# Output and down projection with tokens on the partitions and the weights moving, and a seam to the gate stage by token tile

## The chip, the cores and the metric

The kernel runs on one core of a Trainium2 chip. Its engines work side by side, each through its own list of instructions: PE (TensorE, matmuls; PEld is its load of the operand that stays in the array), DVE (VectorE), ACT (ScalarE), POOL (GpSimd) and SP (SyncE, which here issues the weight loads). The metric is the device time of one execution in microseconds, the median of three runs. The profile is of one execution; its span is the time between the first and the last thing that the profiler saw.

## The reference

One layer over 256 latent tokens of width 2048 (and 256 context tokens that only feed the state of the token mixer). All arithmetic is in float32. What the change touches is the end of the token mixer, the second norm and the feed-forward block:

```python
hx = modulate(rmsnorm(x, norm_mix[l]), sh1, sc1)
x_parts, _, _ = mixer_front(hx, w_in[l], ...)
x = x + g1 * mixer_back(x_parts, ..., w_proj_a[l], w_proj_b[l], w_out[l])   # ends in "@ w_out"
hx = modulate(rmsnorm(x, norm_ffn[l]), sh2, sc2)
x = x + g2 * swiglu(hx, w_ffn_gate[l], w_ffn_up[l], w_ffn_down[l])
...
return rmsnorm(x, norm_final)
```

The vectors sh, sc and g come from SiLU(c) times a matrix w_mod of 2048 by 12288, plus b_mod. w_out is 2048 by 2048, gate and up are 2048 by 5632, down is 5632 by 2048. The mixer's input projection and its state scan come first.

## The kernel before, in words

Every large product is split to keep float32 precision: an operand is taken apart into a rounded part (hi) and the rest (lo), and hi x hi, lo x hi and hi x lo are summed in PSUM. Activations lie with their channels on the partitions: a tile such as `mx` or `h2` holds, for each block of 128 channels, the hi and the lo part of 256 tokens side by side. So one matmul with a 128 by 128 block of weights as the loaded operand and 512 columns moving does hi x hi and lo x hi at once, in two halves of a PSUM bank; one with 256 columns adds the lo part of the weights (`mm_unit`, lines 151 and 153). `fold` then adds the two halves, with a copy on ACT and an addition on DVE.

Weights come in units of 512 KB: `w32` loads a unit with SP (six buffers), `split` makes its hi part on ACT (line 113) and its lo part on DVE (line 114), into four buffers each. `split` is moved some 450 instructions ahead of its place in the program by a priority, so that units are ready before PE asks. `pair` runs one pair of 128 output channels through all units of a weight matrix. With `whole` set it keeps 256 columns to a matmul and needs no fold (lines 143, 144 and 146); this is done for the last pair of the output and of the down projection.

The vectors of the second half (g1, sh2, sc2, g2) are computed beside other stages by `modvec`: DVE multiplies rows of w_mod by one number per partition and sums (line 493), PE adds over the partitions (line 499), ACT copies (501), PE transposes (504), and DVE adds the bias into `modc`, one number per partition. A generator is advanced from `hook`, once per weight unit and by a fixed ratio, so that this work is spread over the stages.

The stages around the change, in order:
- At the start (p0), x is transposed on PE, and ACT copies its 256 token columns to a buffer `ev` from which POOL writes them to `xT_d` (lines 393 and 394), block by block.
- The output projection (pd) has eight calls of `pair`; x comes back from `xT_d`, DVE forms x1 = x + g1 * y (line 951), ACT the squares, and POOL writes x1 to `x1_d`.
- The seam into the gate stage: PE sums the squares over the partitions (line 968) and spreads the scale back over them (976); then DVE, ACT, ACT and DVE make each of 16 blocks of `h2` (lines 978 to 985). The gate stage (pe) starts its first matmuls block by block.
- The down projection (pf) is like the output projection, with x1 read back, and with four transposes per pair (line 1052) that put the result back with tokens on the partitions for the output. The final norm's scale comes at the end (1044 to 1047), then the scaling and the six output writes.

Each engine has one list of instructions, ordered by the program and the priorities; the buffers of a pool are handed on in that order.

## Time and profile before

| | |
|---|---|
| median of 3 runs | 2410.69 us (2408.48 to 2411.11) |
| the profiled execution | 2409.69 us |
| its span | 2407.9 us |
| PE busy | 2346.0 us, 97% of the span |
| DVE busy | 1639.7 us, 68% |
| ACT busy | 1266.5 us, 53% |
| moved by DMA | 509.41 MB, 212 GB/s on average |

Busy times are averages over stages with different limits; the table by stage in the rows below is read first. Durations of matmuls overlap, so their cost is read from the distance between starts.

### The profile page before, as it was taken

The numbers are of one execution on the slowest core, as the hardware profiler recorded it, in microseconds if no ns is written. First come the engines' busy times: TensorE is split into PE (matmuls) and PEld (weight loads), VectorE is DVE, ScalarE is ACT, GpSimd is POOL, SyncE is SP. The second block draws the span as 40 slices with busy tenths as digits, with TensorE's granted clock in tenths as the row PEclk, the third lists the DMA queues.
The fourth block names the chain that finished last, engine by engine and source line by source line (L and its number), as shares of the span: only waits on it lengthen the run. The fifth ranks groups of instructions, "written<-read, shape, count | busy, mean of one in ns | idle before, by whom it ended". The sixth has DMA issues, their size and how long they took to land.

```text
span 2407.9 us, 35235 instructions
## 1 busy us (share of the span) xinstructions
PE 2346.0 (97%) x13400; PEld 1976.3 (82%) x13400; DVE 1639.7 (68%) x2134; ACT 1266.5 (53%) x1980; POOL 131.2 (5%) x165
## 2 busy tenths in 40 slices
...
GB/s 280 289 280 139 134 135 153 160 125 162 136 148 155 163 199 192 266 264 282 246 267 295 261 282 251 276 288 190 219 231 223 210 230 225 222 193 193 192 192 114
DMA packets 468457, 509.41 MB, mean 212 GB/s; under 512 B 18147, under 2 KB 438194, under 8 KB 467776
## 3 DMA queue, kind: packets, MB, share of 16 engines
...
## 4 chain that ended last, share of the span: by engine, by line
PE 84%; DMA 7%; issue 4%; DVE 4%; ACT 2%; POOL 0%; SPq 0%; DVEq 0%; ACTq 0%; POOLq 0%
PE acc L151 38%; PE acc L153 20%; PE acc L143 6%; PE acc L144 6%; PE acc L146 6%; DMA w<-in_w_mod_dram 4%; PE acc L155 2%; DVE wl L114 2%; PE ss L667 1%; DMA cs<-cs_d 1%; PE ss L637 1%; PE tp L558 1%; PE ss L370 1%; DMA w<-in_w_in_dram 1%; DMA yst<-yg_d 1%
## 5 line engine op out<-in xcount | busy, mean ns | idle before, releaser
L114 DVE TENSOR_TENSOR wl<-w,wh 128x1024 fp32r<-128x1024 f32 (+3 forms) x702 | 847.2, 1211 | 486.0 <-ACT wh L113 484.8
L113 ACT CAST wh<-w 128x1024 fp32r<-128x1024 f32 (+3 forms) x702 | 717.0, 1023 | 703.8 <-PE acc L151 459.4
L151 PE MATMUL acc<-hx,wh 128*128 128x512 f32 x1556 | 433.0, 397 | 0.0
L151 PE MATMUL acc<-h,wh 128*128 128x512 f32 x1320 | 366.9, 397 | 4.7 <-DVE h L985 2.4
L151 PEld LDWEIGHTS acc<-hx,wh 128*128 128x128 f32 x1556 | 271.6, 189 | 40.9 <-issue 2.6
L153 PEld LDWEIGHTS acc<-hx,wl 128*128 128x128 f32 x1664 | 254.8, 188 | 35.6
L143 PE MATMUL acc<-hx,wh 128*128 128x512 f32 x656 | 265.7, 406 | 4.1 <-ACT wh L113 3.0
L153 PE MATMUL acc<-hx,wl 128*128 128x256 f32 x1664 | 264.9, 281 | 0.0
L151 PEld LDWEIGHTS acc<-h,wh 128*128 128x128 f32 x1320 | 231.5, 190 | 38.9 <-issue 4.5
L144 PE MATMUL acc<-hx,wh 128*128 128x512 f32 x656 | 259.2, 396 | 0.0
L153 PEld LDWEIGHTS acc<-h,wl 128*128 128x128 f32 x1408 | 215.9, 189 | 30.1
L493 DVE SCALAR_TENSOR_TENSOR mac<-w,silc,mac 128x1024 f32<-128x1024 f32 x120 | 154.7, 1289 | 120.2 <-DMA w<-in_w_mod_dram 119.8
L153 PE MATMUL acc<-h,wl 128*128 128x256 f32 x1408 | 223.7, 281 | 0.0
L146 PE MATMUL acc<-hx,wl 128*128 128x512 f32 x656 | 184.2, 394 | 0.0
L151 PE MATMUL acc<-hid,wh 128*128 128x512 f32 x602 | 166.3, 396 | 0.0
L143 PEld LDWEIGHTS acc<-hx,wh 128*128 128x128 f32 x656 | 123.8, 189 | 39.8 <-ACT wh L113 7.9
L146 PEld LDWEIGHTS acc<-hx,wl 128*128 128x128 f32 x656 | 123.9, 189 | 27.8 <-DVE wl L114 0.8
L144 PEld LDWEIGHTS acc<-hx,wh 128*128 128x128 f32 x656 | 124.2, 189 | 25.7 <-issue 1.6
L151 PE MATMUL acc<-yg,wh 128*128 128x512 f32 x496 | 136.6, 395 | 0.0
L151 PEld LDWEIGHTS acc<-hid,wh 128*128 128x128 f32 x602 | 103.6, 189 | 13.8
L153 PEld LDWEIGHTS acc<-hid,wl 128*128 128x128 f32 x616 | 94.4, 189 | 13.1
L618 ACT ACTIVATE cs<-cs,ncs 128x128 f32<-128x128 f32 x256 | 81.6, 390 | 32.4 <-DMA cs<-cs_d 30.6
...
## 6 DMA issues: line engine op xcount, KB each, us to landing
...
```

The lines of the kernel that those rows point to most:

```text
L113: A.copy(out=hi[:, :n], in_=t[:, :n])
L114: V.tensor_tensor(out=lo[:, :n], in0=t[:, :n], in1=hi[:, :n].bitcast(F32), op=ALU.subtract)
L143: E.matmul(o, wj(hi, k), act(kofs + k)[:, 0, :ncol], start=kofs + k == kbeg, stop=False)
L144: E.matmul(o, wj(hi, k), act(kofs + k)[:, 1, :ncol], start=False, stop=False)
L146: E.matmul(o, wj(lo, k), act(kofs + k)[:, 0, :ncol], start=False, stop=last and k == nk - 1)
L151: E.matmul(o2, wj(hi, k), act(kofs + k)[:, :, :T], start=kofs + k == kbeg, stop=False)
L153: E.matmul(o[:, :T], wj(lo, k), act(kofs + k)[:, 0, :T], start=False, stop=last and not hold)
L155: E.matmul(o2, wj(hi, nk - 1), act(kofs + nk - 1)[:, :, :T], start=False, stop=True)
L370: E.matmul(b[32 * j:32 * j + 32, :fb], sil[:, rr, :], wt[:, r, :], start=rr < 4, stop=rr >= KD - 4)
L493: V.scalar_tensor_tensor(out=ac, in0=wt, scalar=silc[:, k - 1:k], in1=ac, op0=ALU.mult, op1=ALU.add)
L558: E.transpose(out=b[:, i * P:(i + 1) * P], in_=v, identity=ident)
L618: A.activation(out=t4[:, r, j], in_=t4[:, r, j], func=AF.Identity, bias=ncs[:, cc, r * 64 + hs + j:r * 64 + hs + j + 1])
```

## The change

- The output and the down projection have the activations as the loaded operand and the weights moving: a PSUM tile holds 128 tokens by up to 512 output channels. The 2048 output channels go in chunks of 512, 512, 512, 256 and 256 (`CHUNKS`), and a unit holds 2 or 4 blocks of 128 input channels (`mm_tok`, `chunks`). There is no fold and no transpose of the down projection's result.
- g1 and g2 are needed along the free dimension now: `modvec` writes them as a row to `gr_d`, adds the bias before the sum over the partitions, and skips the transposes for them; they are read back spread over all partitions. `modvec` has one more step in each half, between the copy and what follows.
- x is read where it is needed, from the input; `xT_d` and its writes at the start are gone. x1 and the output are token by channel.
- Norms: squares are summed along the free dimension by the instruction that makes them, with one scale per partition.
- The seam: the last chunk of the output projection runs all its units for token tile 0 first, then for tile 1 with the same held weight buffers. The norm of a tile (`norm2`) scales, transposes on PE and evicts with scale and bias, four blocks at a time. The first four gate units run for tile 0 and then, again with held buffers, for tile 1 (`mm_half`), ahead of the up units.

```diff
+CHUNKS = (512, 512, 512, 256, 256)
...
-    xT_d = dpool.tile([P, KD, T], F32, name="xT_d")
-    x1_d = dpool.tile([P, KD, T], F32, name="x1_d")
+    x1_d = dpool.tile([T, D], F32, name="x1_d")
+    gr_d = dpool.tile([2, D], F32, name="gr_d")
...
+    def mm_half(a, hi, lo, nk, kofs, kend, act, tt):
+
+        s = slice(tt * P, (tt + 1) * P)
+        for j in range(2):
+            o = a[j].rearrange("p (h t) -> p h t", h=2)[:, :, s]
+            wj = lambda t, k: t[:, k, j * P:(j + 1) * P]
+            for k in range(nk):
+                E.matmul(o, wj(hi, k), act(kofs + k)[:, :, s], start=kofs + k == 0, stop=False)
+            for k in range(nk):
+                E.matmul(o[:, 0], wj(lo, k), act(kofs + k)[:, 0, s], start=False, stop=kofs + k == kend - 1)
+
+    def mm_tok(a, hi, lo, nk, kofs, kend, act, tt):
+
+        s = slice(tt * P, (tt + 1) * P)
+        o = a[tt][:, :UB // nk]
+        for k in range(nk):
+            E.matmul(o, act(kofs + k)[:, 0, s], hi[:, k], start=kofs + k == 0, stop=False)
+            E.matmul(o, act(kofs + k)[:, 1, s], hi[:, k], start=False, stop=False)
+        for k in range(nk):
+            E.matmul(o, act(kofs + k)[:, 0, s], lo[:, k], start=False, stop=kofs + k == kend - 1)
+
+    def chunks(w, ktot, act, epi, hook=None, split=False):
+
+
+        c0 = 0
+        for j, n in enumerate(CHUNKS):
+            a, nk = acc2(), UB // n
+            held = []
+            for k in range(0, ktot, nk):
+                u = (*unit_cols(w, k, nk, [(c0, n)]), nk, k, ktot, act)
+                for tt in range(1 if split and j == len(CHUNKS) - 1 else 2):
+                    mm_tok(a, *u, tt)
+                held.append(u)
+                if hook is not None:
+                    hook()
+            epi(a, 0, j, c0, n)
+            if split and j == len(CHUNKS) - 1:
+                for u in held:
+                    mm_tok(a, *u, 1)
+            epi(a, 1, j, c0, n)
+            c0 += n
...
-                xo = p0.tile([P, 512], F32, tag="ev", name="ev", bufs=2)[:, :T]
-                A.copy(out=xo, in_=b[:, :T])
-                nc.gpsimd.dma_start(out=xT_d[:, k, :], in_=xo)
...
+            if slot in (0, 3):
+                br = w32([(lambda t: t[0:1, :], b_mod[0][c0:c0 + UB].rearrange("(a n) -> a n", a=1))])
...
                     V.tensor_scalar(out=ac, in0=wt, scalar1=silc[:, 0:1], scalar2=None, op0=ALU.mult)
+                    if slot in (0, 3):
+                        V.tensor_tensor(out=ac[0:1, :], in0=ac[0:1, :], in1=br[0:1, :], op=ALU.add)
...
             A.copy(out=ev, in_=b[:, :w])
+            yield
+            if slot in (0, 3):
+                nc.gpsimd.dma_start(out=gr_d[slot // 3, h * UB:(h + 1) * UB].rearrange("(j n) -> j n", j=4),
+                                    in_=ev.rearrange("(j r) n -> j r n", j=4)[:, 0, :])
+                continue
...
-    hook = bg(mgen, 102, 226)
+    hook = bg(mgen, 108, 226)
...
-        x1 = pd.tile([P, KD, T], F32, name="x1")
-        ss2 = pd.tile([P, 2, T], F32, name="ss2")
-        for j in range(8):
-            xr = pd.tile([P, 2, T], F32, tag="xr", name="xr", bufs=2)
-            nc.gpsimd.dma_start(out=xr, in_=xT_d[:, 2 * j:2 * j + 2, :])
-            a = pair(w_out, j * 256, KD, lambda k: mx[:, k], hook, whole=j == 7)
...
-            if j < 7:
-                fold(a, t)
...
-                v = (ss2, t)[i // 2][:, i % 2, tt * P:(tt + 1) * P]
-                E.matmul(b[:, 2 * tt:2 * tt + 2], v, ones[:, 0:2], start=i == 0, stop=i == 3)
...
+        x1 = [pd.tile([P, D], F32, name=f"x1{i}") for i in range(2)]
+        g1 = pd.tile([P, D], F32, name="g1")
+        sq = pd.tile([P, 2, len(CHUNKS)], F32, name="sq")
+        rs2 = pd.tile([P, 2], F32, name="rs2")
+        nc.gpsimd.dma_start(out=g1, in_=gr_d[0].partition_broadcast(P))
+        xr = {}
+
+        def xload(j):
+            c0, n = sum(CHUNKS[:j]), CHUNKS[j]
+            xr[j] = pd.tile([P, 2, 512], F32, tag="xr", name="xr", bufs=2)
+            nc.gpsimd.dma_start(out=xr[j][:, :, :n], in_=x[:, c0:c0 + n].rearrange("(t p) n -> p t n", p=P))
+
+        def norm2(tt):
+
+            r = rs2[:, tt:tt + 1]
+            V.tensor_reduce(out=r, in_=sq[:, tt, :], op=ALU.add, axis=mybir.AxisListType.X)
+            A.activation(out=r, in_=r, func=AF.Sqrt, scale=1.0 / D, bias=eps_t)
+            V.reciprocal(out=r, in_=r)
+            for k0 in range(0, KD, 4):
+                xn = pd.tile([P, 512], F32, tag="xn", name="xn", bufs=2)
+                V.tensor_scalar(out=xn, in0=x1[tt][:, k0 * P:k0 * P + 512], scalar1=r, scalar2=None, op0=ALU.mult)
+                b = tpb()
+                for i in range(4):
+                    E.transpose(out=b[:, i * P:(i + 1) * P], in_=xn[:, i * P:(i + 1) * P], identity=ident)
+                h = pd.tile([P, 4, P], F32, tag="h32", name="h32", bufs=2)
+                for i in range(4):
+                    k = k0 + i
+                    bi = b[:, i * P:(i + 1) * P]
+                    if i % 2:
+                        A.activation(out=h[:, i, :], in_=bi, func=AF.Identity, scale=modc[:, 2, k:k + 1],
+                                     bias=modc[:, 1, k:k + 1])
+                    else:
+                        V.tensor_scalar(out=h[:, i, :], in0=bi, scalar1=modc[:, 2, k:k + 1],
+                                        scalar2=modc[:, 1, k:k + 1], op0=ALU.mult, op1=ALU.add)
+                hh, hl = (h2[:, k0:k0 + 4, i, tt * P:(tt + 1) * P] for i in range(2))
+                A.copy(out=hh, in_=h)
+                V.tensor_tensor(out=hl, in0=h, in1=hh.bitcast(F32), op=ALU.subtract)
+
+        def epi(a, tt, j, c0, n):
+            last = j == len(CHUNKS) - 1
+            if tt == 0 and not last:
+                xload(j + 1)
+            if tt == 0 and last:
+                for _ in mgen:
+                    pass
+            cs = slice(c0, c0 + n)
+            xc, xt = x1[tt][:, cs], xr[j][:, tt, :n]
+            V.tensor_tensor(out=xc, in0=a[tt][:, :n], in1=g1[:, cs], op=ALU.mult)
+            V.tensor_tensor(out=xc, in0=xc, in1=xt, op=ALU.add)
+            if last:
+                V.scalar_tensor_tensor(out=xt, in0=xc, scalar=1.0, in1=xc, op0=ALU.mult, op1=ALU.mult,
+                                       accum_out=sq[:, tt, j:j + 1])
             else:
...
+                A.activation(out=xt, in_=xc, func=AF.Square, accum_out=sq[:, tt, j:j + 1])
+            nc.gpsimd.dma_start(out=x1_d[tt * P:(tt + 1) * P, cs], in_=xc)
+            if last:
+                norm2(tt)
+        xload(0)
+        chunks(w_out, KD, lambda k: mx[:, k], epi, hook, split=True)
...
-        hook = bg(mgen, 34, 168)
+        hook = bg(mgen, 36, 168)
+        h2a = lambda k: h2[:, k]
         for j in range(KF // 2):
             ag, au = acc2(), acc2()
+            if j == 0:
+                held = []
+                for k0 in range(0, KD, UK):
+                    held.append((*unit_cols(w_gate, k0, UK, [(0, 256)]), UK, k0, KD, h2a))
+                    mm_half(ag, *held[-1], 0)
+                    hook()
+                for u in held:
+                    mm_half(ag, *u, 1)
             for k0 in range(0, KD, UK):
                 for w, a in ((w_gate, ag), (w_up, au)):
-                    hi, lo = unit_cols(w, k0, UK, [(j * 256, 256)])
-                    mm_unit(a, hi, lo, UK, k0, KD, [0, 0], lambda k: h2[:, k])
-                    hook()
+                    if j or a is au:
+                        hi, lo = unit_cols(w, k0, UK, [(j * 256, 256)])
+                        mm_unit(a, hi, lo, UK, k0, KD, [0, 0], h2a)
+                        hook()
...
-            a = pair(w_down, j * 256, KF, lambda k: hid[:, k], whole=j == 7)
-            t = pf.tile([P, 2, T], F32, tag="ff", name="ff", bufs=2)
-            if j < 7:
-                fold(a, t)
...
+        g2 = pf.tile([P, D], F32, name="g2")
+        nf = pf.tile([P, D], F32, name="nf")
+        sq = pf.tile([P, 2, len(CHUNKS)], F32, name="sq3")
+        rs = pf.tile([P, 2], F32, name="rsf")
+        nc.gpsimd.dma_start(out=g2, in_=gr_d[1].partition_broadcast(P))
+        nc.gpsimd.dma_start(out=nf, in_=norm_final.partition_broadcast(P))
+        for tt in range(2):
+            nc.gpsimd.dma_start(out=ot[tt], in_=x1_d[tt * P:(tt + 1) * P, :])
+
+        def epi3(a, tt, j, c0, n):
+            last = j == len(CHUNKS) - 1
+            cs = slice(c0, c0 + n)
+            o = ot[tt][:, cs]
+            t = pf.tile([P, 512], F32, tag="ff", name="ff", bufs=2)[:, :n]
+            V.tensor_tensor(out=t, in0=a[tt][:, :n], in1=g2[:, cs], op=ALU.mult)
+            V.tensor_tensor(out=o, in0=o, in1=t, op=ALU.add)
+            if last:
+                V.scalar_tensor_tensor(out=t, in0=o, scalar=1.0, in1=o, op0=ALU.mult, op1=ALU.mult,
+                                       accum_out=sq[:, tt, j:j + 1])
             else:
...
+                A.activation(out=t, in_=o, func=AF.Square, accum_out=sq[:, tt, j:j + 1])
+                V.tensor_tensor(out=o, in0=o, in1=nf[:, cs], op=ALU.mult)
+        chunks(w_down, KF, lambda k: hid[:, k], epi3)
+        V.tensor_reduce(out=rs, in_=sq, op=ALU.add, axis=mybir.AxisListType.X)
+        A.activation(out=rs, in_=rs, func=AF.Sqrt, scale=1.0 / D, bias=eps_t)
+        V.reciprocal(out=rs, in_=rs)
...
+                    V.scalar_tensor_tensor(out=ot[tt][:, m:], in0=ot[tt][:, m:], scalar=r, in1=nf[:, m:], op0=ALU.mult,
+                                           op1=ALU.mult)```

How the instructions stand, at three places. First PE where a gate vector is summed over the partitions, for g1. Before (`mac` is the vector, `ident` the operand of a transpose; L151, L153 and L155 are matmuls of the projection that runs there):

```order
L155 MATMUL acc<-hx,wh 128x512
L499 MATMUL tp<-mac,ones 32x256 x4
L151 MATMUL acc<-hx,wh 128x512 x4
L153 MATMUL acc<-hx,wl 128x256
L504 MATMUL tp<-ident,mac 128x128 x2
L153 MATMUL acc<-hx,wl 128x256 x3
```

The same place now (L543 is the sum over the partitions; L152, L154 and L156 are the old L151, L153 and L155):

```order
L156 MATMUL acc<-hx,wh 128x512
L543 MATMUL tp<-mac,ones 32x256 x4
L152 MATMUL acc<-hx,wh 128x512 x4
L154 MATMUL acc<-hx,wl 128x256 x4
L152 MATMUL acc<-hx,wh 128x512 x4
```

The two transposes of this half have gone.

Second, PE at the seam. Before, from the last matmuls of the output projection (L146) over the sums and the spread scale to the first gate matmuls (`h_13993` is `h2`):

```order
L146 MATMUL acc<-mx,wl 128x256 x4
L968 MATMUL tp<-ones,ss_13998 128x2 x2
L968 MATMUL tp<-ones,fd 128x2 x2
L968 MATMUL tp<-ones,ss_13998 128x2 x2
L968 MATMUL tp<-ones,fd 128x2 x2
L976 MATMUL tp<-dg,ones 128x128 x2
L151 MATMUL acc<-h_13993,wh 128x512 x10
L153 MATMUL acc<-h_13993,wl 128x256 x4
```

Now, from inside the last unit of token tile 1 (L174, L175 and L177 are `mm_tok`, L1012 the transposes of `norm2`, L165 and L167 `mm_half`, `h_13945` is `h2`):

```order
L174 MATMUL acc<-wh,mx 128x256
L1012 MATMUL tp<-ident,xn 128x128 x8
L175 MATMUL acc<-wh,mx 128x256
L174 MATMUL acc<-wh,mx 128x256
L175 MATMUL acc<-wh,mx 128x256
L174 MATMUL acc<-wh,mx 128x256
L175 MATMUL acc<-wh,mx 128x256
L174 MATMUL acc<-wh,mx 128x256
L175 MATMUL acc<-wh,mx 128x256
L177 MATMUL acc<-wl,mx 128x256 x4
L1012 MATMUL tp<-ident,xn 128x128 x8
L165 MATMUL acc<-h_13945,wh 128x2x128 x4
```

Two sets of eight transposes stand ahead of the first gate matmul, the second directly ahead of it. Those of token tile 1 stand inside the gate units of tile 0.

Third, DVE at the same place, now, from the last operation of tile 0's epilogue on (L115 is the lo split of a weight unit, L1009 the normalised block `xn`, L1021 an eviction of a transposed block, L1036 the epilogue of tile 1, L1025 the lo part of `h2`):

```order
L1039 SCALAR_TENSOR_TENSOR xr,sq<-x_13949 128x256
L1004 TENSOR_REDUCE rs_13953<-sq 128x1
L115 TENSOR_TENSOR wl<-w_14860,wh 128x1024
L1006 RECIPROCAL rs_13953<-rs_13953 128x1
L1009 TENSOR_SCALAR xn<-x_13949,rs_13953 128x512 x2
L115 TENSOR_TENSOR wl<-w_14882,wh 128x1024
L115 TENSOR_TENSOR wl<-w_14904,wh 128x1024
L1021 TENSOR_SCALAR h_14685<-tp,modc 128x128
L1021 TENSOR_SCALAR h_14699<-tp,modc 128x128
L115 TENSOR_TENSOR wl<-w_14926,wh 128x1024
L1021 TENSOR_SCALAR h_14685<-tp,modc 128x128
L1021 TENSOR_SCALAR h_14699<-tp,modc 128x128
```

Before, the reciprocal had one split ahead of it, and the blocks of `h2` followed it:

```order
L114 TENSOR_TENSOR wl<-w_15045,wh 128x1024
L971 RECIPROCAL rs_14891<-rs_14891 128x4
L975 TENSOR_SCALAR dg<-ident,rs_14891 128x128 x2
L978 SCALAR_TENSOR_TENSOR x_13997<-x_13997,modc,tp 128x256 x2
L981 TENSOR_SCALAR x_13997<-x_13997,modc 128x256
L978 SCALAR_TENSOR_TENSOR x_13997<-x_13997,modc,tp 128x256 x2
L985 TENSOR_TENSOR h_13993<-x_13997,h_13993 128x256 x2
```

All four gate units' splits stand among the operations of tile 0's norm now, three ahead of its first evictions and the fourth between them.

## Rows read from the trace of the kernel before

**Rows 1.** Busy time by stage: engine busy us (instructions), granted clock, DMA share, GB/s.

```profile
0.00:180.00 180.00, 146.51 (x1068) 99.64 (x1069) 95.18 (x200) 65.64 (x139) 18.11 (x41) 0.96 0.92 283
...
1553.00:1637.00 84.00, 82.77 (x508) 73.17 (x508) 57.79 (x75) 37.89 (x52) 8.05 (x15) 1.00 0.85 269
...
1637.00:1656.00 19.00, 15.11 (x79) 12.91 (x79) 15.36 (x34) 13.61 (x29) 0.55 (x1) 0.82 0.40 123
...
2145.00:2396.40 251.40, 251.40 (x1524) 222.86 (x1523) 126.11 (x139) 103.95 (x123) 4.00 (x8) 1.00 0.56 176
```

**Rows 2.** DMA of the first 180 us: bytes; one issue group (count, KB, landing us).

```profile
DMA packets 54219, 50.95 MB, mean 283 GB/s; under 512 B 2470, under 2 KB 53167, under 8 KB 53693
...
xT_d<-ev POOLq DMA_DIRECT2D x14, 128.0 KB, 5.3
```

**Rows 3.** Waits in the first 180 us: waiter <- waited for: us, times, longest.

```profile
ACT ev L374 <- DMA xT_d<-ev: 4.3, 2, 3.6
```

**Rows 4.** Groups by line, PE, whole span: busy us, mean ns, idle before, releaser.

```profile
L504 PE MATMUL tp<-ident,mac 128*128 128x128 f32 x16 | 3.2, 279 | 3.3 <-ACT mac L501 3.3
```

**Rows 5.** PE in order of time, 410 to 2192 us: start, us, instruction.

```profile
411.44 0.39 PE L144 MATMUL acc<-hx,wh 128*128 128x512 f32 x1
...
413.98 0.84 PE L151 MATMUL acc<-hx,wh 128*128 128x512 f32 x3
...
2180.26 0.70 PE L1052 MATMUL tp<-ident,xr 128*128 128x128 f32 x4
...
2180.72 0.72 PE L153 MATMUL acc<-hid,wl 128*128 128x256 f32 x4
...
2182.19 0.64 PE L153 MATMUL acc<-hid,wl 128*128 128x256 f32 x4
...
2182.66 1.09 PE L151 MATMUL acc<-hid,wh 128*128 128x512 f32 x4
...
2190.61 0.64 PE L153 MATMUL acc<-hid,wl 128*128 128x256 f32 x4
```

**Rows 6.** PE in order of time at the seam into the gate stage.

```profile
1636.25 0.64 PE L146 MATMUL acc<-mx,wl 128*128 128x256 f32 x4
...
1638.17 0.59 PE L968 MATMUL tp<-ones,ss 128*128 128x2 f32 x4
...
1638.62 0.59 PE L968 MATMUL tp<-ones,fd 128*128 128x2 f32 x4
...
1643.30 4.60 PE L151 MATMUL acc<-h,wh 128*128 128x512 f32 x10 [2.44 <-DVE h L985]
...
1647.71 0.67 PE L153 MATMUL acc<-h,wl 128*128 128x256 f32 x4
```

**Rows 7.** Groups by line, PE, from 1636.5 to 1655.24 us.

```profile
L151 PE MATMUL acc<-h,wh 128*128 128x512 f32 x29 | 10.2, 480 | 2.4 <-DVE h L985 2.4
...
L153 PE MATMUL acc<-h,wl 128*128 128x256 f32 x28 | 4.5, 282 | 0.0
```

**Rows 8.** Groups by line, DVE, from 1300 us on.

```profile
L114 DVE TENSOR_TENSOR wl<-w,wh 128x1024 fp32r<-128x1024 f32 x378 | 460.0, 1222 | 299.2 <-ACT wh L113 298.6 <-PE acc L151 0.4
...
L896 DVE TENSOR_TENSOR mx<-fc,mx 128x512 fp32r<-128x512 f32 x8 | 5.5, 683 | 0.0
...
L951 DVE SCALAR_TENSOR_TENSOR x<-fd,modc,xr 128x256 f32<-128x256 f32 x14 | 6.8, 484 | 4.9 <-DMA xr<-xT_d 4.5
...
L1064 DVE TENSOR_SCALAR ot<-ot,rsf 128x512 f32<-128x512 f32 x2 | 1.0, 484 | 0.0
...
L975 DVE TENSOR_SCALAR dg<-ident,rs 128x128 f32<-128x128 f32 x2 | 0.5, 284 | 0.0
```

**Rows 9.** Groups by line, ACT, from 1300 us on.

```profile
L113 ACT CAST wh<-w 128x1024 fp32r<-128x1024 f32 x378 | 395.8, 1050 | 460.6 <-PE acc L151 344.2 <-PE acc L155 46.7 <-issue 32.3
```

**Rows 10.** Order of time at the end, PE and DVE.

```profile
2395.78 0.64 PE L146 MATMUL acc<-hid,wl 128*128 128x256 f32 x4
...
2399.28 1.41 DVE L1064 TENSOR_SCALAR ot<-ot,rsf 128x512 f32<-128x512 f32 x3
```

78 lines of the change are left out of this document (5 added, 73 removed).

## The prediction

> **What bounds the kernel now.** I read the table by stage first. TensorE (PE) is the bound: in the down projection it is busy for all of 251.4 us, in the output projection for 82.8 of 84 us [rows 1]. Two stretches differ. In the first 180 us PE is busy for 146.5 us while the DMA engines are at 0.92: there the bytes set the pace. Between the output projection and the first full-speed gate matmuls PE waits for VectorE (DVE). So I asked three things: what a matmul costs in the new form, what the two seams (into the gate stage, and to the end) cost PE, and what becomes of the DMA traffic of the first 180 us. After the stages I read the DMA queues of the first stretch, PE in order of time at one place of each form, and the seam in order of time.
>
> **The matmuls.** Back to back, eleven 512-column matmuls take 413.98 - 411.44 = 2.54 us, 0.231 each; four 256-column ones take 0.47, 0.12 each [rows 5]. A unit in the old form (8 of 512 and 8 of 256 columns) is 2 x (2190.61 - 2182.19)/6 = 2.807 us [rows 5]. In the new form a 512-column chunk has 12 matmuls of 512 columns a unit, 2.772; a 256-column chunk has 24 of 256, 2.88, which is also what the last pair costs now. Which operand is loaded and which moves makes no difference to the row I can see; the columns do. Output projection before: 28 x 2.807 + 4 x 2.88 = 90.1; after: 24 x 2.772 + 8 x 2.88 = 89.6: **-0.5**. Down projection before: 77 x 2.807 + 11 x 2.88 = 247.8, after: 66 x 2.772 + 22 x 2.88 = 246.3: -1.5. It also loses its transposes: four took 2180.72 - 2180.26 = 0.46 of PE's time, seven such sets lay between matmuls, -3.2 [rows 5]. Down in all **-4.7**; PE is never idle there, so this comes off the path whole. Bounds: if a 512-column matmul with moving weights went at 0.234, both stages would gain nothing from the form, +3.
>
> **The gate vectors.** The rows for g1 and g2 are no longer transposed on PE. The sixteen transposes of line 504 cost 0.115 each of PE's time and 3.3 us of idle time for the copy just before them [rows 4]. Eight of them go; the other eight now stand a hook later, with matmuls in between, as the order shows. -0.9 and -3.3: **-4.2**, or -0.9 if the idle time only moves to the next weights. Added on DVE are four additions on one partition and on the weight queue four 4 KB loads that hold one of six buffers each for two hooks. They lie beside matmuls that have four split units in hand; I cost them at nothing, +1 if that cover is thin. The two new writes of a gate row sit between two uses of the one "mac" buffer; the next use comes a hook later (about 6 us), against 5.3 us for a write on that queue [rows 2].
>
> **The first 180 us.** The write of the transposed x goes: 14 writes of 128 KB in this stretch are 1.8 MB of 50.95 MB. At 283 GB/s that is 6.5 us [rows 2]. A copy on ScalarE (ACT) also waited 4.3 us for such a write [rows 3]. With the engines at 0.92 most of it should come off the path. I take **-5**; bounds 0, if the stretch is paced by the latency of six buffers and not by bytes, and -6.5.
>
> **The start of the output projection.** g1 (1 MB) and the first x rows (512 KB) are loaded on the POOL queue, where two loads of 256 KB went before. The stage runs at 269 GB/s and a DMA share of 0.85 [rows 1]. Before, DVE stood 4.5 us waiting for such a load in front of weight splits [rows 8]; now the first epilogue is eight units (22 us) later and its data are there. Against that, 1 MB more is 4 us of full bandwidth. I take **0**; bounds -1.7 and +4. In the down stage 4 MB come at once on that queue, at a DMA share of 0.56 and 60 us ahead of their use: nothing.
>
> **The seam.** Before: from the last output matmul (1636.73, four at 0.12 after 1636.25) to 1655.24, 18.5 us, PE got through 29 matmuls of 512 and 28 of 256 columns, worth 10.06 us [rows 6, 7]. **The old seam costs 8.5 us**, part of it because the clock was granted at 0.82 on average over the stretch [rows 1]: the first ten gate matmuls begin 4.41 us ahead of the next ones [rows 6]. After: take zero at the end of the last output matmul of token tile 0. PE has 48 matmuls of 256 columns of tile 1 left, 5.8 us, and all four weight buffers are held by them. DVE, in the order that the program has: two operations on 256 elements and the square (0.48 each by the nearest row), the split of the first gate unit (1.22; its cast, 1.05 on ACT, has to wait until tile 1 has used the first held buffer), reciprocal near 4.0, two normalised blocks (0.48 each) to 5.1, two more splits to 7.5, four evictions (0.28 each) around a further split to 10.0, two more blocks to 11.0 [rows 8, 9]. PE has by then done eight transposes and finished tile 1 at 6.9; the next in its order are the transposes of block 2, ready at 10.5: 3.6 us idle. The first gate matmul needs the low part of block 0, behind another epilogue operation (0.48) and a 0.68 us subtraction: 12.1. From there eight half units. One has 8 matmuls of 256 columns and 8 of 128. The 128-column matmul in this type is not in the trace. Bounds are 0.06 (half of 0.12) and 0.12. The nearest row is one whose columns count for nothing: the two-column matmuls, each behind its own load, start four in 1638.62 - 1638.17 = 0.45, 0.112 each [rows 6]. I take 0.115, which makes a half unit 1.88 and eight 15.0. With 16 transposes of tile 1 (1.8) and 1.3 us of waiting for its first block this ends at 30.2. PE's work in it at the old price is 5.8 + 4 x 2.807 = 17.0. **The new seam costs 13.2 us, +4.7.**
>
> The Trainium skill ("TensorE: Matmul & The Clock Gate", section "Back-to-back issue gap") gives about 81 ns for a 128-column matmul with its load in a stream. By that figure a half unit would be an estimated 1.61 us, the seam 2 us shorter and the sum -12.1. The 0.112 of the row speaks against it, though for another type; no run here shows the 128-column one.
>
> Bounds of the seam: DVE's work alone in it (epilogues 2.9, blocks 3.9, evictions 4.5, subtractions 5.5, splits 4.9) is 21.7; with one half unit behind it, 23.6 - 17.0 = 6.6, that is -1.9. The other end is below.
>
> **The end.** From the last matmul's end (2396.42) to the first scaling (2399.28) it is 2.86 us [rows 10]. After: three DVE operations (0.48 each), a small reduction, root and reciprocal (an estimate of 0.8 with the hand-overs), some 2.3 us; the matmuls with ones go. **-0.6**, bounds -1 and +0.5.
>
> **Sum**: -0.5 - 4.7 - 4.2 - 5 + 0 + 4.7 - 0.6 = -10.3. The profiled execution took 2409.7 us (its span is 2407.9), so 2399.4; the median of the runs is 1.0 above it, so I forecast **2400.4 us**.
>
> **Rivals.**
> 1. *The first stretch gains nothing* (its pace is the round trip of six buffers, and the bytes removed leave holes). For: a weight load can only be issued when one of six buffers has been freed, by PE or by a split. Against: a DMA share of 0.92. Then 2405.4. Chance 0.20.
> 2. *The seam overlaps as it is laid out*: DVE is never late for a reason other than its own work, seam 6.6. For: half of the gate's work can start with token tile 0. Against: the splits stand ahead of the evictions in DVE's order. Then 6.6 less, 2393.8. The 81 ns of the skill's page would take the seam part of the way there. Chance 0.18.
> 3. *Slower: the clock stays at its lower level through the seam.* Place: PE between the end of the output projection and the first whole gate unit. Before, the rate fell to 0.44 us for a 512-column matmul (4.41 us for ten, against 0.231) after it had stood idle, and came back on a dense stream of long matmuls [rows 6]. Now the idle time is followed by short matmuls with waits between them. If the eight half units go at half rate they take 30 us instead of 15: +15 on the sum, 2415.4. It decides from a mean granted clock below 0.7 over the seam. Chance 0.12.
> 4. My forecast: 0.50, with its own range 2394 to 2407.
>
> That the change doesn't do what it says I don't count: the order shows the new forms in their places.
>
> **How the numbers follow.** A measurement of this kernel tells some 0.2%, 4.8 us, from no change: faster is below 2405.9, slower above 2415.5. Faster: 0.9 of the forecast, all of rival 2, a little under half of rival 1 (it lies at that border): 0.45 + 0.18 + 0.09 = 0.72. Slower: half of rival 3 and a tail of its neighbours, 0.08. The rest, 0.20, is no change. The range 2391 to 2411 takes rival 2 with a full gain in the first stretch, and rival 1 with an uncovered load at the start of the output projection; what is left out is mostly rival 3.
>
> **What would show it.** PE's last matmul of the first stretch's projections earlier by 5 us; no idle time at the gate vectors' transposes; twelve matmuls a unit at 0.231 in the down stage and none of the transposes; in the seam an idle PE of 3 to 4 us ahead of its second group of transposes, and 128-column matmuls 0.11 to 0.12 apart. I am wrong if the down stage is not shorter by 4 to 5 us, if the seam costs PE less than 9 us, or if the first 180 us keep their length.

## The result, and the profile after

The changed kernel takes 2398.2 us in the median of 7 runs (2393.1 to 2402.9), the kernel before 2410.7 in 7 runs beside it: a ratio of 0.9947 (95% interval 0.9932 to 0.9962). The forecast was 2400.4. The profiled execution took 2399.29 us, its span is 2397.6, 10.3 less than before. That this is also the forecast's sum is chance: two of its terms were wrong by 4.4 and 5 us, in opposite directions.

The table by stage of the kernel after (columns as in [rows 1]; the cuts are those of the table further down):

```profile
0.00:180.00 180.00, 147.09 (x1070) 100.38 (x1071) 95.81 (x201) 61.50 (x125) 10.47 (x27) 0.97 0.89 274
...
1625.79:1656.29 30.50, 26.41 (x211) 25.65 (x209) 25.72 (x52) 20.39 (x36) 1.08 (x2) 0.94 0.34 102
...
2144.01:2387.07 243.06, 243.06 (x1321) 212.00 (x1319) 120.35 (x118) 97.05 (x105) 2.14 (x4) 1.00 0.57 191
```

TensorE (PE) is busy all through the down projection, 243.06 us, where it took 252.2 before. The first 180 us have a DMA share of 0.89 where it was 0.92, and PE is busy for 147.1 us, no more than the 146.5 of [rows 1].

The DMA of these 180 us, answering to [rows 2]:

```profile
DMA packets 53729, 49.29 MB, mean 274 GB/s; under 512 B 2253, under 2 KB 53126, under 8 KB 53204
```

The bytes fell from 50.95 to 49.29 MB, and the rate with them, 283 to 274 GB/s: the engines were left emptier and nothing came earlier. The first matmul of the gating stage, the end of this stretch, starts at 237.9 us after 238.4.

PE by line: the transposes of the gate vectors, answering to [rows 4]; they now wait for nothing.

```profile
L553 PE MATMUL tp<-ident,mac 128*128 128x128 f32 x8 | 1.5, 272 | 0.0
```

PE in order of time in the down projection, answering to [rows 5]; a row is start, duration, instruction:

```profile
2184.39 0.61 PE L177 MATMUL acc<-wl,hid 128*128 128x512 f32 x2
...
2185.75 0.61 PE L177 MATMUL acc<-wl,hid 128*128 128x512 f32 x2
```

Six matmuls of 512 columns, a pair and four single ones, start every 1.36 us: 0.2267 each, not the 0.231 that the forecast took. A unit is 2.72 us. The kernel before had this price too, in other runs of the lines that [rows 5] shows:

```profile
183.13 0.39 PE L144 MATMUL acc<-hx,wh 128*128 128x512 f32 x1
...
186.31 0.39 PE L144 MATMUL acc<-hx,wh 128*128 128x512 f32 x1
```

Between these two starts lie fourteen matmuls of 512 columns in 3.18 us, 0.227 each. The eleven of [rows 5] were a slower run; why isn't known.

PE in order of time at the seam, answering to [rows 6]:

```profile
1625.79 0.28 PE L174 MATMUL acc<-wh,mx 128*128 128x256 f32 x1
...
1632.21 0.64 PE L177 MATMUL acc<-wl,mx 128*128 128x256 f32 x4
1635.98 1.85 PE L1012 MATMUL tp<-ident,xn 128*128 128x128 f32 x8 [3.13 <-ACT h L1018]
1637.48 1.20 PE L165 MATMUL acc<-h,wh 128*128 128x256 f32 x4
...
1655.89 0.56 PE L167 MATMUL acc<-h,wl 128*128 128x128 f32 x4
1656.29 1.14 PE L152 MATMUL acc<-h,wh 128*128 128x512 f32 x4
```

Token tile 0's last output matmul ends at 1625.79. From there the transposes for tile 0's later blocks begin at 10.2 us (forecast 10.5), the first gate matmul at 11.7 (12.1), the first matmuls of a whole unit at 30.5 (30.2). The 3.13 us of idle time stand where the forecast put 3.6. VectorE (DVE) in the same stretch shows why:

```profile
1630.67 2.35 DVE L115 TENSOR_TENSOR wl<-w,wh 128x1024 fp32r<-128x1024 f32 x2
1632.94 0.72 DVE L1021 TENSOR_SCALAR h<-tp,modc 128x128 f32<-128x128 f32 x2
1633.59 1.22 DVE L115 TENSOR_TENSOR wl<-w,wh 128x1024 fp32r<-128x1024 f32 x1
1634.72 0.72 DVE L1021 TENSOR_SCALAR h<-tp,modc 128x128 f32<-128x128 f32 x2
```

The splits of the held gate units (L115, 2.35 and 1.22 us) stand before and between the first four evictions (L1021).

The end, answering to [rows 10]:

```profile
2386.43 0.64 PE L177 MATMUL acc<-wl,hid 128*128 128x256 f32 x4
...
2389.22 1.55 ACT L1123 ACTIVATE ot<-ot,rsf 128x512 f32<-128x512 f32 x2 [0.23 <-DVE rsf L1116]
```

PE's last matmul ends at 2387.07, the scaling starts 2.15 us later (forecast 2.3, before 2.86).

Below are stage lengths in us, read from the same places of all traces: the first matmul of the gating stage; the first output matmul; the end of token tile 0's last output matmul (6.42 us ahead of tile 1's last group of low-part matmuls, where rows are merged); the first 512-column matmul of a whole unit behind the half units; the first and the last matmul of the down projection; the end of the span. In e2, where the two tiles alternate, the third cut is 5.74 us ahead of the end of the last output matmul, so that the same work lies behind it. The names are those of the experiments.

| kernel | first stretch | scans, branches | output proj., to tile 0's end | seam | gate, up | down | end |
|---|---|---|---|---|---|---|---|
| before | 238.4 | 1305.5 | 600.3 for these three | | | 252.2 | 11.5 |
| after | 237.9 | 1302.0 | 85.9 | 30.5 | 487.7 | 243.1 | 10.5 |
| e1_writes_back | 236.0 | 1301.4 | 88.3 | 30.5 | 486.4 | 243.1 | 10.5 |
| e2_plain_seam | 235.5 | 1301.0 | 87.4 | 521.3 for both | | 243.1 | 10.5 |
| e3_down_256 | 235.1 | 1301.2 | 88.6 | 31.9 | 488.7 | 253.6 | 10.5 |
| e4_down_512 | 234.3 | 1299.1 | 90.9 | 31.9 | 488.2 | 239.5 | 12.3 |
| e5_before_gap | 234.3 | 1298.6 | 599.5 for these three | | | 263.6 with the end | |
| e6_late_split | 236.3 | 1303.2 | 87.4 | 29.1 | 488.0 | 243.1 | 10.5 |
| e8_small_loads | 236.2 | 1302.3 | 85.4 | 30.5 | 488.1 | 243.1 | 10.4 |
| e9_best | 237.7 | 1301.7 | 83.6 | 29.1 | 486.8 | 239.5 | 8.6 |
| e10_seventh | 227.0 | 1298.1 | 85.3 | 29.1 | 486.9 | 239.5 | 8.7 |
| e11_no_gap | 235.7 | 1309.3 | 91.4 | 31.8 | 490.1 | 243.1 | 10.5 |
| e12_pace_only | 234.4 | 1308.7 | 83.6 | 30.5 | 487.9 | 243.1 | 10.5 |

The down projection repeats to 0.1 us; the first stretch of the same code varies by 3.6 us from trace to trace, so a single pair of traces says little there. The output projection varies too: 85.9 to 90.9 us in the kernel after, e3, e4 and e6, whose code is the same up to the seam.

### The profile page after: what moved, and what is told of

Read it like the earlier page. It is cut to its first block, busy times and chain, and to the rows that moved or that the text cites. A ratio compares the mean times of both kernels' runs of the same rounds, so it can differ in the third digit from the quotient of the medians.

```text
span 2397.6 us, 34659 instructions
## 1 busy us (share of the span) xinstructions
PE 2337.8 (98%) x13180; PEld 1968.7 (82%) x13180; DVE 1633.7 (68%) x2099; ACT 1252.8 (52%) x1934; POOL 126.9 (5%) x149
## 3 DMA queue, kind: packets, MB, share of 16 engines
q10 hardware_dynamic: 560, 1.08, 0.1%
## 4 chain that ended last, share of the span: by engine, by line
PE 89%; DMA 5%; DVE 2%; ACT 2%; issue 1%; SPq 1%; DVEq 0%; ACTq 0%
PE acc L152 34%; PE acc L154 18%; PE acc L144 6%; PE acc L145 5%; PE acc L147 5%; PE acc L177 4%; PE acc L174 4%; PE acc L175 4%; DMA w<-in_w_mod_dram 3%; PE acc L156 2%; DMA w<-in_w_in_dram 2%; PE ss L716 1%; PE ss L413 1%; DMA cs<-cs_d 1%; PE ss L686 1%
## 5 line engine op out<-in xcount | busy, mean ns | idle before, releaser
L115 DVE TENSOR_TENSOR wl<-w,wh 128x1024 fp32r<-128x1024 f32 (+3 forms) x702 | 847.1, 1210 | 486.6 <-ACT wh L114 484.4
L114 ACT CAST wh<-w 128x1024 fp32r<-128x1024 f32 (+3 forms) x702 | 717.7, 1024 | 742.2 <-PE acc L152 349.6
L152 PE MATMUL acc<-hx,wh 128*128 128x512 f32 x1556 | 433.0, 397 | 0.0
L152 PE MATMUL acc<-h,wh 128*128 128x512 f32 x1290 | 356.6, 395 | 1.9 <-DVE fe L204 1.9
L152 PEld LDWEIGHTS acc<-hx,wh 128*128 128x128 f32 x1556 | 271.9, 189 | 40.8 <-issue 2.2
L154 PEld LDWEIGHTS acc<-hx,wl 128*128 128x128 f32 x1664 | 254.8, 188 | 37.6 <-DVE wl L115 2.1
L144 PE MATMUL acc<-hx,wh 128*128 128x512 f32 x656 | 266.3, 407 | 3.0 <-ACT wh L114 2.6
L154 PE MATMUL acc<-hx,wl 128*128 128x256 f32 x1664 | 265.1, 281 | 1.4 <-DVE wl L115 1.4
L152 PEld LDWEIGHTS acc<-h,wh 128*128 128x128 f32 x1290 | 225.5, 189 | 34.0 <-DVE fe L204 2.6
L154 PEld LDWEIGHTS acc<-h,wl 128*128 128x128 f32 x1376 | 211.5, 189 | 29.7
L154 PE MATMUL acc<-h,wl 128*128 128x256 f32 x1376 | 219.5, 281 | 0.0
L144 PEld LDWEIGHTS acc<-hx,wh 128*128 128x128 f32 x656 | 124.2, 189 | 38.1 <-ACT wh L114 8.2
L175 PE MATMUL acc<-wh,hid 128*128 128x512 f32 (+1 forms) x440 | 146.8, 347 | 0.0
L174 PE MATMUL acc<-wh,hid 128*128 128x512 f32 (+1 forms) x440 | 146.8, 347 | 0.0
L152 PE MATMUL acc<-yg,wh 128*128 128x512 f32 x496 | 136.3, 395 | 0.0
L177 PE MATMUL acc<-wl,hid 128*128 128x512 f32 (+1 forms) x440 | 109.5, 347 | 0.0
```

The costliest lines, as they stand in the source:

```text
L114: A.copy(out=hi[:, :n], in_=t[:, :n])
L115: V.tensor_tensor(out=lo[:, :n], in0=t[:, :n], in1=hi[:, :n].bitcast(F32), op=ALU.subtract)
L144: E.matmul(o, wj(hi, k), act(kofs + k)[:, 0, :ncol], start=kofs + k == kbeg, stop=False)
L152: E.matmul(o2, wj(hi, k), act(kofs + k)[:, :, :T], start=kofs + k == kbeg, stop=False)
L154: E.matmul(o[:, :T], wj(lo, k), act(kofs + k)[:, 0, :T], start=False, stop=last and not hold)
L174: E.matmul(o, act(kofs + k)[:, 0, s], hi[:, k], start=kofs + k == 0, stop=False)
```

## The experiments

All ratios are to the kernel before, run beside each, with the 95% interval.

**The first stretch: bytes or buffers.** e1 puts the writes back:

```
+ xo = p0.tile([P, 512], F32, tag="ev", name="ev", bufs=2)[:, :T]
+ A.copy(out=xo, in_=b[:, :T])
+ nc.gpsimd.dma_start(out=xT_d[:, k, :], in_=xo)
```

> The changed kernel with one part undone: the transposed x is copied on ScalarE and written to memory again in the first stretch (16 writes of 128 KB that nothing reads). Theory (the first 180 us are paced by the round trip of the six weight buffers, so bytes removed only leave the engines emptier): the first matmul of the stage behind it begins at 237.9 us as without the writes, give or take 1 us, the DMA rate over 0 to 180 us goes back from 274 to about 283 GB/s, and the time is that of the changed kernel. Rival (bytes set the pace): that matmul begins 5 us later, the kernel is 5 us longer, a ratio of 0.997.

Measured 2399.1 us, 0.9952 (0.9940 to 0.9965); the stretch is 236.0 us, inside the spread without the writes (e5 below, which has them too, shows 234.3). Its DMA in the first 180 us:

```profile
DMA packets 55456, 51.93 MB, mean 288 GB/s; under 512 B 2507, under 2 KB 54404, under 8 KB 54930
```

The rate is up again at the same length: the removed bytes were worth nothing. e7 takes away a weight buffer instead:

```
- NW32, NWH, NWL = 6, 4, 4
+ NW32, NWH, NWL = 5, 4, 4
```

> The changed kernel with five buffers for weights on their way instead of six, throughout. Only the first stretch is read: from the start to the first matmul of the gating stage, 234.3 to 237.9 us in the traces of the four kernels that share it. Theory (its pace is the round trip of the weight buffers): 49.3 MB in 180 us with six buffers become slower by up to a fifth, the first stretch is 10 to 36 us longer and the DMA rate in it falls well below 274 GB/s. Rival (the DMA engines' bandwidth sets the pace): the stretch stays within 2 us and the rate at 270 to 275 GB/s.

One run, 2431.5 us. Its DMA of the first 180 us, and the end of the stretch (matmul count, durations, first and last start):

```profile
DMA packets 49653, 46.02 MB, mean 256 GB/s; under 512 B 2130, under 2 KB 49050, under 8 KB 49128
```

```profile
L352 PE MATMUL tp<-xt,s_gt x6: 221/275/275, 249.8 to 251.2; 128*128 128x64 f32 x6
```

The stretch is 249.8 us, 13.9 longer than the mean of the nine traces with six buffers and without the writes (235.9). The waits of the weight queue in the kernel after, over 0 to 240 us (us, times, longest), say the same: it stands nearly half the time for a buffer that PE or DVE has still to free.

```profile
SPq L107 <- PE ss L413: 55.4, 37, 5.7
SPq L107 <- DVE wl L115: 52.6, 28, 6.5
```

**The down projection: width.** e3 makes all chunks 256 wide, e4 all 512 (for the down projection alone):

```
+ C3 = (256,) * 8        # e3;  (512,) * 4 in e4
- chunks(w_down, KF, lambda k: hid[:, k], epi3)
+ chunks(w_down, KF, lambda k: hid[:, k], epi3, CHUNKS=C3)
  # and the sizes in epi3 and behind it go by C3
```

> The changed kernel with the down projection in eight chunks of 256 columns. Theory (its gain is a matter of width: 0.2267 us for a matmul of 512 columns, 0.12 for one of 256, so that a unit costs 2.88 us instead of 2.72, and 66 units are made narrow): TensorE's stretch from the first to the last matmul of that stage grows by 66 x 0.16 = 10.6 us, from 243.1 to 253.6, the end stays as it is, and the time is 10.6 us longer than the changed kernel's: about the time of the kernel before, a ratio of 0.999. Rival (the gain was in the form, the operand that moves, and in the transposes that went, not in the width): the stretch stays within 3 us of 243.1.

> The changed kernel with the down projection in four chunks of 512 columns instead of three of 512 and two of 256. Theory (a unit costs 2.72 us in matmuls of 512 columns, 2.88 in matmuls of 256): the 22 units of the two narrow chunks lose 0.16 each, TensorE's last matmul ends 3.5 us earlier; the last epilogue works on 512 columns instead of 256, so the end grows by 1 to 1.8 us; in all 2 us shorter than the changed kernel, a ratio to the kernel before of about 0.994. Rival (the width makes no difference, only the transposes and the fold that went did): TensorE's end stays within 1 us and the kernel is 1 to 2 us longer through its end.

e3: 2410.8 us, 1.0006 (0.9991 to 1.0020). PE there, twelve matmuls of 256 columns every 1.44 us:

```profile
2201.05 0.64 PE L178 MATMUL acc<-wl,hid 128*128 128x256 f32 x4
...
2202.49 0.64 PE L178 MATMUL acc<-wl,hid 128*128 128x256 f32 x4
```

e4: 2397.8 us, 0.9942 (0.9929 to 0.9956), not told apart from the changed kernel by time.

By the traces both sums hold: 253.6 and 239.5 us for the stage, where 253.6 and 239.6 were expected, and 1.8 us more for the end of e4. In e3, with all chunks narrow, the stage is 1.4 us longer than in the kernel before, though it has no transposes: the matmuls gain nothing without width. By the same prices the 9.1 us that the change gains in this stage are about 3.9 for the seven sets of transposes (0.56 each, see below) and 4.9 for the matmuls: 66 units at 2.72 instead of 2.807, less 11 more units at 2.88.

**The seam.** e2 takes the work by token tile out:

```
- chunks(w_out, KD, lambda k: mx[:, k], epi, hook, split=True)
+ chunks(w_out, KD, lambda k: mx[:, k], epi, hook)
  # and the first gate chunk in whole units, no mm_half
```

> The changed kernel with one part undone: the last chunk of the output projection takes both token tiles unit by unit, and the first gate chunk waits for both tiles (no half units). Theory (with norms on tokens there are 32 transposes, their evictions and subtractions between the two stages, 20 us of VectorE, and only the work by token tile hides part of it): TensorE is idle for most of 14 us between the last output matmul and the first gate matmul, and the run is 1 to 5 us longer than the changed kernel, about 3, a ratio of 0.995 to 0.997. Rival (the half units and the held weights are themselves the cost of the seam): 5 us shorter than the changed kernel, as cheap as the seam of the kernel before, a ratio of 0.9925.

Measured 2401.7 us, 0.9963 (0.9951 to 0.9975), 3.9 us above the changed kernel by the two ratios, as expected. PE at its seam:

```profile
1629.13 0.64 PE L177 MATMUL acc<-wl,mx 128*128 128x256 f32 x4
1633.14 1.94 PE L1012 MATMUL tp<-ident,xn 128*128 128x128 f32 x8 [3.37 <-issue]
1636.42 2.12 PE L1012 MATMUL tp<-ident,xn 128*128 128x128 f32 x8 [1.34 <-ACT h L1018]
1641.53 1.97 PE L1012 MATMUL tp<-ident,xn 128*128 128x128 f32 x8 [2.99 <-ACT h L1018]
1646.28 1.97 PE L1012 MATMUL tp<-ident,xn 128*128 128x128 f32 x8 [2.77 <-ACT h L1018]
1647.90 1.99 PE L152 MATMUL acc<-h,wh 128*128 128x512 f32 x4
```

PE stands idle for 10.5 us ahead of the four groups of transposes, and does nothing useful but these from 1629.61 to 1647.90. e6 takes the high priority off the splits of the held gate units:

```
- held.append((*unit_cols(w_gate, k0, UK, [(0, 256)]), UK, k0, KD, h2a))
+ held.append((*unit_cols(w_gate, k0, UK, [(0, 256)], 0), UK, k0, KD, h2a))
  # last argument: the priority offset of the split, 450 elsewhere
```

> The changed kernel, but the splits of the four held gate units lose their high priority, so that in the seam two of the three splits that stood ahead of VectorE's evictions now come behind the first of them. Theory (the seam is paced by the order of VectorE's work: TensorE's second group of transposes comes at 10.2 us because the splits of 1.2 us each stand ahead of the evictions that it needs): the idle time of 3.1 us ahead of that group shrinks to about 1, the first gate matmul comes at about 9.5 us instead of 11.7, full-speed matmuls begin 1 to 3 us earlier than 30.5, and the run is 1 to 3 us shorter than the changed kernel: a ratio to the kernel before of 0.9935 to 0.9943 instead of 0.9947. Rival (the total of VectorE's work sets the seam, not its order): the idle time only moves to a later group, the full-speed matmuls begin at 30 to 31 us again, no gain.

Measured 2395.2 us, 0.9931 (0.9917 to 0.9945). Its seam:

```profile
1633.31 0.64 PE L177 MATMUL acc<-wl,mx 128*128 128x256 f32 x4
1635.16 0.66 PE L1012 MATMUL tp<-ident,xn 128*128 128x128 f32 x4 [1.21 <-ACT h L1018]
1636.87 0.74 PE L165 MATMUL acc<-h,wh 128*128 128x256 f32 x4 [1.05 <-DVE h L1025]
...
1656.01 1.14 PE L152 MATMUL acc<-h,wh 128*128 128x512 f32 x4
```

The idle time ahead of the second transposes is 1.21 us, the first gate matmul comes 10.0 us after tile 0's end (1626.89), and whole units begin at 29.1 instead of 30.5. Part of the saved 1.9 us is given back in a wait of 1.05 for DVE. By the trace the gain is 1.4 us; the times, 3.9 us apart by the two ratios, with intervals that overlap, can't tell that from nothing.

**The start of the output projection.** e8 cuts up the loads for the epilogue:

```
- nc.gpsimd.dma_start(out=g1, in_=gr_d[0].partition_broadcast(P))
+ nc.gpsimd.dma_start(out=g1[j][:, :n], in_=gr_d[0, c0:c0 + n].partition_broadcast(P))
  # in xload(j); one buffer for g1 and for xr; xload(j + 1) behind the epilogue of chunk j
```

> The changed kernel with the loads for the output projection's epilogue cut up: the gate row g1 comes chunk by chunk (256 KB beside the x rows of that chunk), with one buffer each, so that a chunk's loads start when the chunk before has been added up. At the start of the stage 768 KB are loaded on the POOL queue instead of 2 MB (g1 whole and the x rows of two chunks). Theory (those 2 MB take bandwidth from the weights, and TensorE waits for late weight splits: 1.7, 2.9, 5.1, 2.8 and 2.9 us in the five traces that have them, 3.1 in the mean): the idle time at the start falls below 1 us, the stage from its first matmul to the last of token tile 0 takes 84 to 85.5 us instead of 85.9 to 89.5 (87.7 in the mean), and the run is some 2.5 us shorter than the changed kernel, a ratio of 0.993 to 0.994. Rival (the rows for the gate vectors or the weights themselves set the waits at that place): the idle time stays at 2 to 3 us and the time is unchanged.

Measured 2396.9 us, 0.9944 (0.9928 to 0.9960). PE's wait there, beside that of e4, which has the large loads:

```profile
PE acc L177 <- DVE wl L115: 1.6, 1, 1.6
```

```profile
PE acc L178 <- DVE wl L116: 5.1, 2, 3.3
```

e4 has the longest such wait. In the changed kernel it is 1.7 us, hardly more than in e8, and in the six traces with the large loads and the change's pace and step (after, e1, e2, e3, e4, e6) 1.7 to 5.1. The stage takes 85.4 us, at the upper end of what was expected, and 83.6 and 85.3 in e9 and e10 below, which have the edit too: 84.8 in the mean, against 88.1 (85.9 to 90.9) in those six. But the idle time did not go below 1 us, the time is that of the changed kernel, and e12 below, which has the large loads, takes 83.6 with no such wait. So the large loads alone do not make it; that they cost something where they meet the rows of the gate vectors is a guess that wasn't tried.

**The gate vectors.** e5 puts the further step between the sum and the transposes into the kernel before, with the pace that goes with it:

```
  A.copy(out=ev, in_=b[:, :w])
+ yield
...
- hook = bg(mgen, 102, 226)
+ hook = bg(mgen, 108, 226)
...
- hook = bg(mgen, 34, 168)
+ hook = bg(mgen, 36, 168)
```

> The kernel before, with one part of the change alone: a further step between the sum over partitions of a gate vector and its transposes, which then stand a hook later, with matmuls between; all sixteen transposes stay. Theory (the change's gain between the scans and the output projection comes from the idle time of 3.3 us ahead of these transposes and from the eight that went, 0.9 us): no idle time at the transposes, the stretch from the first matmul of the gating stage (238.4 us in the trace of before) to the first matmul of the output projection is 1303 us instead of 1305.5, and the time is 2 to 3.3 us shorter than before, a ratio of 0.9987 or a little more. Rival (the idle time moves to the next weights, the gain was made by the transposes and their weight loads or by other loads that went): the stretch keeps its 1305.5 us and the ratio is 1.000.

Measured 2403.5 us, 0.9969 (0.9956 to 0.9981): 7.5 us, more than the 3.3 that the theory could explain. The stretch from the gating stage to the output projection is 1298.6 us, where the theory had 1303. Its sixteen transposes do wait for nothing, as the theory said:

```profile
L505 PE MATMUL tp<-ident,mac 128*128 128x128 f32 x16 | 3.1, 272 | 0.0
```

e11 takes step and pace out of the changed kernel, e12 the step alone:

```
- yield
- hook = bg(mgen, 108, 226)    # these two lines in e11 alone
+ hook = bg(mgen, 102, 226)
  # and 36 of 168 back to 34 in e11
```

> The changed kernel with one part undone: the further step between the sum over partitions of a gate vector and what follows it is taken out again, so that the eight transposes left come right behind the sum, as in the kernel before. That step alone, put into the kernel before, had made it 0.9969 [0.9956, 0.9981] of its time, 7.5 us, where the idle time at the transposes is 3.3 us. Theory A (the step is worth what its waits show): with eight of the sixteen transposes left the idle time ahead of them is back at 1 to 3 us in the stages up to the output projection, and the time is 1 to 3.5 us longer than the changed kernel, a ratio of 0.995 to 0.996. Theory B (each such wait also delays the weight splits and casts behind it, so that the step is worth twice what is shown at the transposes): the stretch from the first matmul of the gating stage to the first of the output projection, 1301.6 us in the mean of seven traces, becomes 1304 to 1306, and the time is 4 to 7 us longer than the changed kernel, a ratio of 0.9965 to 0.9975.

> The changed kernel without the further step, as in the run before, but with the change's pace of the background work (108 steps in 226 hooks and 36 in 168, instead of 102 and 34), which comes with the step in the change. Theory P (the pace: it sets at which hooks a row of the gate vectors' weights is asked for and multiplied, and so how long VectorE stands waiting for rows in front of weight splits): the time is that of the changed kernel, a ratio of 0.994 to 0.996, and the stretch from the first matmul of the gating stage to the first of the output projection is 1301 to 1303 us. Theory S (the step: it keeps the transposes and what follows from standing right behind the sum): the time is that of the kernel without the step, a ratio of 1.000 to 1.002, and the stretch is 1307 to 1310 us.

e11: 2414.5 us, 1.0016 (1.0003 to 1.0028), slower than the kernel before, and far over both theories. PE's waits in it, over the whole span (us, times, longest), and the same of the kernel after:

```profile
PE acc L154 <- DVE wl L115: 6.1, 6, 1.8
PE acc L177 <- DVE wl L115: 5.7, 2, 4.5
PE acc L152 <- DVE fe L204: 4.3, 1, 4.3
...
PE tp L552 <- ACT mac L545: 0.7, 1, 0.7
```

```profile
PE acc L152 <- DVE fe L204: 1.9, 1, 1.9
PE acc L177 <- DVE wl L115: 1.7, 1, 1.7
PE acc L154 <- DVE wl L115: 1.4, 1, 1.4
```

The wait at the transposes (L552) is 0.7 us; those for weight splits (wl) and sums (fe) grew from 5.0 to 16.1. So what is lost does not stand at the transposes. e12: 2402.9 us, 0.9969 (0.9956 to 0.9982), between the two:

```profile
PE acc L154 <- DVE wl L115: 4.8, 4, 2.3
...
PE acc L152 <- DVE fe L204: 3.2, 2, 2.8
```

Pace alone brings 0.47% of the 0.69% by the ratios, the step the rest, 0.22%, which is little more than its uncertainty. The step acts in the stretch before the output projection, 1308.7 us in e12 and 1302.0 after. That stretch, e12 and then the kernel after (columns as in [rows 1]):

```profile
234.39:1543.05 1308.66, 1294.93 (x7100) 1087.05 (x7098) 977.31 (x1252) 768.46 (x1276) 104.49 (x100) 1.00 0.69 207
```

```profile
237.92:1539.92 1302.00, 1293.33 (x7099) 1087.67 (x7098) 974.84 (x1249) 771.13 (x1276) 103.07 (x100) 1.00 0.69 207
```

PE is idle for 13.7 us of it without the step and 8.7 with it. In the same way it is idle for 12.1 to 13.7 us in the three traces without the step (before, e11, e12) and 6.0 to 9.0 in the ten that have it and six or more buffers, e5 among them: the step, in e5 together with the pace, is worth some 5 us there in either kernel. Where the pace acts can't be said: e11 and e12 differ in the output projection (91.4 and 83.6) and the gate stage (490.1 and 487.9), but these are single traces, and the first of the two varies by 5 us in the same code. Theory B was nearer, but neither foresaw the size, and of P and S neither holds alone. Which wait delays which split isn't settled: the pace sets at which hooks a weight row is asked for and multiplied, and DVE's waits for rows between 1000 and 2160 us are 129.2 us in e11, 109.3 in e12, 104.0 after; that these are the cause is argued, not shown.

**Better versions.** e9 joins e4, e6 and e8 and lets token tile 0 finish first at the end:

```
+ hold = split and j == len(CHUNKS) - 1 and k + 4 * nk >= ktot
+ for tt in range(1 if hold else 2):
      mm_tok(a, *u, tt)
  # and in epi3, behind the last chunk: norm, scaling and output of tile tt alone
```

> The changed kernel with three edits of the runs before together (splits of the held gate units without their priority, loads of the output projection's epilogue by chunk, down projection in four chunks of 512 columns), and one more: the last four units of the down projection take token tile 0 first, so that its norm, scaling and output lie beside tile 1's matmuls, and only tile 1's stand behind the last matmul. Theory (the gains lie in different stages of one chain on TensorE and add up): down 3.5 us shorter (239.5 from its first matmul to its last), seam 1.4 us shorter (29.1 us from the end of tile 0 to the first full-speed matmuls), the output projection at 85.4 us up to the end of tile 0, 2.3 us better than the mean of those without that edit, the end 10.5 us or less instead of 12.3 with the wide last chunk; in all some 7 us shorter than the changed kernel, a ratio to the kernel before of 0.992. Rival (gains given back: what comes earlier only waits later, as for weights): 2 to 3 us shorter than the changed kernel, a ratio of 0.9935 or more.

Measured 2386.9 us, 0.9899 (0.9883 to 0.9916). The end of e9:

```profile
2372.97 0.69 DVE L1122 TENSOR_TENSOR ff<-acc,g 128x512 f32<-128x512 f32 x1 [3.58 <-PE acc L178]
...
2377.76 0.61 PE L178 MATMUL acc<-wl,hid 128*128 128x512 f32 x2
...
2381.32 0.94 ACT L1110 ACTIVATE ot<-ot,rsf 128x768 f32<-128x768 f32 x1 [0.23 <-DVE rsf L1108]
```

Tile 0's last epilogue starts 4.8 us ahead of the last matmul group; tile 1's scaling starts 2.95 us behind the last matmul. The gains add up, to more than expected: down 3.5, seam 1.4, output projection 2.3 (no more than e12 has without the edit of e8) and end 1.9 us less than in the changed kernel's trace, 9.1 together; by the ratios it is 0.48%, 11.6 us. e10 adds a seventh weight buffer in the first stretch:

```
+ if more[0] is not None and more[1] % (NW32 + 1) == 0:
+     t = more[0].tile([P, UB], F32, tag="w33", name="w33", bufs=1)
```

> The kernel of the run before this one with a seventh buffer for weights on their way, in the first stretch alone; room is made by taking one buffer each from two small kinds of temporary (three to two, two to one), which can cost a little. Theory (the first stretch is paced by the round trip of the weight buffers: five instead of six cost 13.9 us): the first matmul of the gating stage comes 3 to 9 us before 236 us (the mean of the traces with six), the DMA rate over 0 to 180 us rises above 280 GB/s, and the time falls by as much, a ratio 0.001 to 0.004 lower than without it. Rival (at six the DMA engines, at 0.88 to 0.92 of their time, are what limits): within 2 us of 236 us, or later where the fewer temporaries are missed.

Measured 2377.9 us, 0.9866 (0.9851 to 0.9881), the fastest of all: 32 us under the kernel before, 20 under the changed one.

```profile
DMA packets 58624, 52.06 MB, mean 289 GB/s; under 512 B 2403, under 2 KB 58020, under 8 KB 58098
```

```profile
L360 PE MATMUL tp<-xt,s_gt x6: 221/275/275, 227.0 to 228.4; 128*128 128x64 f32 x6
```

The stretch ends at 227.0 us, 8.9 ahead of the mean with six buffers, at 289 GB/s. Five, six and seven buffers give 249.8, 235.9 and 227.0.

## Why the prediction came out right

The likeliest case and its number were right, its working only in part. By its terms:

- **Down projection, forecast -4.7, measured -9.1.** Mechanism right, size off. The 0.231 for a 512-column matmul came from one run of eleven in [rows 5]; other runs in the same trace go at 0.227, and so do the new units (0.2267). That is 66 x 0.052 = 3.4 of the 4.4 us. And a set of transposes cost the kernel before 0.56 rather than 0.46: the unit with them took 3.36 us there (2178.83 to 2182.19) against 2.80; 0.7 us for seven.
- **First 180 us, forecast -5, measured 0.** The step that failed: "With the engines at 0.92 most of it should come off the path." A high DMA share was read as bytes setting the pace. e1 and e7 show that the round trip of the buffers does. This was the mechanism of rival 1, given 0.20.
- **Gate vectors, forecast -4.2.** The two traces differ by 3.5 us in the stretch before the output projection, and PE is idle there for 3.4 us less; but the size came near by luck. The forecast counted the eight transposes and the 3.3 us of idle time shown at them. In e11 the wait at the transposes is 0.7 us, and PE is idle in that stretch for 13.6 us, no less than the 12.1 of the kernel before: the lost time stands elsewhere. By the times, step and pace together are worth some 16 us to this kernel, and without them the change would have been slower than the kernel before. Put into the kernel before they give 7.5 us (e5), more than half of the whole gain. Against e5 the change brings only 0.22%, 5.3 us, little more than the uncertainty, which agrees with the traces: down and end 10.1 us shorter, the seam 5.0 dearer. What the rest of the change costs without step and pace was costed at nothing, +1 if the cover is thin, and is some 8 us: e11 is 3.9 us slower than before by the ratio, though its down projection, end and seam together are 3.8 us shorter. The gate row's two 4 KB loads, which hold one of six buffers for two hooks, are the candidate, and they weren't tried alone.
- **Start of the output projection, forecast 0, waits of 1.7 to 5.1 us there.** The expectation of 1.5 MB on the POOL queue was itself short: the x rows of two chunks are asked for at once, 2 MB with g1. Whether these loads make the waits isn't settled (e8 and e12). The stage's own gain was larger than the -0.5 forecast (24 units at 2.72 instead of 2.772, another -1.2).
- **Seam, forecast +4.7.** Right, and so were its checkpoints: 13.5 us (30.5 less 17.0 of PE's work) against 8.5 before, +5.0. A 128-column matmul takes (1656.29 - 1655.89)/4 = 0.10, between the 0.115 taken and the lower bound. The Trainium skill's 81 ns ("TensorE: Matmul & The Clock Gate", section "Back-to-back issue gap") does not agree with this trace. (By that figure the prediction's sum would have been an estimated -12.5, not the -12.1 that it gives: eight half units at 1.61 instead of 1.88 are 2.2 us less.) Rival 2 did not come: DVE's order mattered, by 1.4 us in e6.
- **Rival 3 (the clock stays low)** came in small. In the kernel after, the seam had a granted clock of 0.94 and the lower level ended within the first half unit; in e4 it lasted for the first two (four matmuls of 256 columns in 0.96 us, half the rate, the 1.2 GHz level) and the seam took 31.9; in e1 there was none, and it took 30.5 as in the kernel after. So it is worth 1.4 us at most, not 15. The tables of e4 and then e1 over 1626 to 1657 us (the granted clock is the third number from the end):

```profile
1626.00:1657.00 31.00, 27.05 (x199) 26.01 (x198) 24.28 (x47) 20.69 (x37) 0.62 (x2) 0.89 0.37 113
```

```profile
1626.00:1657.00 31.00, 25.54 (x211) 24.42 (x210) 25.58 (x52) 21.20 (x37) 1.08 (x2) 1.00 0.35 110
```

- **End, forecast -0.6, measured -1.0.**

So the sum was right because down gave 4.4 us more than forecast and the first stretch 5 less, and because step and pace hid what else the change costs. Of the three signs that the prediction named for being wrong, one came: the first 180 us kept their length. The down projection was shorter not by the 4 to 5 us that another sign named, but by twice as much.
